# Queries and keys of three retention heads in seven products, tables made late, and a few steps moved

## The chip, the core and the metric

The kernel runs on one NeuronCore of a Trainium2 chip. The metric is the device time of one launch in microseconds (us); smaller is better. TensorE is PE in the rows, its weight loads PEld, VectorE DVE, ScalarE ACT, GpSimd POOL, and SyncE, which issues most transfers, SP.

## What is computed

One decoder layer on 512 tokens of width 1024, batch 1, everything in float32. Two branches read the same normalised input: latent attention with eight heads, and retention with four heads (queries and keys 256 wide, values and gates 512 wide). Their gated sum goes through an output projection, then come a squared-ReLU MLP and a gated embedding.

```python
h = rms_norm(x, norm_mix); proj = h @ w_in
rq, rk, rv, rg, cq, ckv, krope, gr, gm = split(proj)
rq = rope(rq, pos); rk = rope(rk, pos) * 256 ** -0.5
ro = retention(rq, rk, rv)            # causal scores times a decay, per head
a_ret = (rms_norm(ro) * silu(rg)) @ w_br
a_mla = latent_attention(cq, ckv, krope, pos) @ w_bm
x = x + (sigmoid(gr) * a_ret + sigmoid(gm) * a_mla) @ w_o
x = x + square(relu(rms_norm(x) @ w_up)) @ w_down
x = x + sigmoid(rms_norm(x) @ w_ple_gate) * (p @ w_ple)
```

## The kernel before

Features lie on the 128 partitions and tokens along the free side. A float32 product is made of three products in the format fp32r: each operand is split into a high part and a rest, and low by high, high by low and high by high are added in PSUM (`mm3`, all under L169). So each 128x512 product costs three matmuls.

All weights are streamed in chunks, mostly 128x1024 (512 KB). SP loads a chunk into a raw tile `wr_...` (six of them, NRAW), ScalarE copies the high part into `wh_...` (L262), VectorE subtracts to get the rest `wl_...` (L266); three such pairs exist. `load_chunk` does this one chunk ahead of the chunk in use (AHEAD 1), `prepare` issues loads three ahead (PREP 3). The program is a list of steps in a fixed order (`step(key, fn, ...)`); `run_steps` walks it. TensorE and the transfers follow the order in which this is written; on the other engines a scheduler may place instructions in another order, unless an instruction is pinned with `keep_in_program_order`.

Values and gates of retention (`rv`, `rg`), for two heads at a time (a pair `q`), and the MLP are done by a scheme with seven half-size products instead of eight, numbered 1, 7, 2, 6, 5, 4, 3. For it, sums of weight blocks are needed. They are made by transfers: product 7's chunk is loaded by SP, then POOL issues a transfer that adds a second block onto it; for products 6 and 4 POOL adds further blocks onto the same raw tile, which it can do only after `wl_` of the product before has read that tile. Product 5's chunk is likewise a load plus an addition. `XS[p]` holds the matching sums of the input. `seven_out` collects the seven results out of three PSUM chains (a: 1, 6, 5, 3; c: 7, 4; b: 2).

Queries and keys of each head are made by `ret_qk` in four chunks (rq 0, rq 1, rk 0, rk 1), each of 24 matmuls 128x512, then turned by the tables `cr`, `sr` (cosine, sine) on VectorE. `ret_scores` makes scores (`rs`), `ret_attend` the outputs (`ro`) and the sum of squares; `ret_gated` multiplies output, root and gate (four VectorE operations, `o`), `ret_turned` transposes that through PSUM (`ot`, sixteen TensorE transposes) and splits the four PSUM tiles into `rog0h`, `rog0l` and so on (ScalarE, then VectorE); `branch_r` multiplies by `w_br` (`br`). PSUM has eight banks, all handed out by one pool (`B(...)`).

Before retention come the first products (`pA`), latents, eight attention heads, and the products with `w_bm` (`bm`). During attention, chunks of the gate projection (`gm`) serve as fillers: `fill(n)` puts n of them into the list of steps at that place. The tables of retention are made between `pair_stats` and the first head factors:

```python
    step(None, pair_stats, 0)
    fill(2)
    step(None, ret_angles)
    step(None, ret_sincos)
    step(None, head_factor, 0)
```

The MLP begins with `up` chunks in the plain form, then `dn` and `us` chunks in seven products; `up_operand` splits the sums of the normalised input (`xu6h`, `xu2h`, ...) for the later `us` products.

## Time and profile before

| | |
|---|---|
| time before, median of 3 runs | 1102.07 us (1100.86 to 1102.21) |
| the profiled execution, its own time | 1101.0 us |
| its span in the profile | 1099.2 us |
| TensorE busy | 1085.2 us, 99% |
| VectorE busy | 757.9 us, 69% |
| ScalarE busy | 565.8 us, 51% |
| GpSimd busy | 111.1 us, 10% |
| granted TensorE clock, mean | 0.999 |

Times in a trace count from the start of the span; the profiled execution took 1.8 us more than its span, and the median of the runs is 1.1 us above the profiled execution. Matmuls are pipelined and their ends are modelled, so what one costs is the distance from its start to the next start, not its duration.

### The profile page before, as it was taken

To read this page: it belongs to the slowest core of one execution; us is meant where nothing else is said; L and a number is where in the kernel's file an instruction comes from. 1 tells how busy PE (TensorE), PEld (TensorE's weight loads), DVE (VectorE), ACT (ScalarE), POOL (GpSimd) and SP (SyncE) were. 2 spreads that over 40 slices of the span, in tenths; PEclk is the share of its full clock that TensorE was granted. 3 is DMA by queue.
4 is the path that set the end of the run, shared out by engine and by line. 5 is a ranking of instruction groups with operands and counts; after the bars stand their busy time and mean duration, and the time that the engine had idled before them with its cause. 6 is when DMAs were issued, how large, how long until landed. Compare 5 with 4: busy or idle time off the path is not lost. (4 is left out here: it accounts for less than half of the span.)

```text
span 1099.2 us, 14887 instructions
## 1 busy us (share of the span) xinstructions
PE 1085.2 (99%) x5569; PEld 923.3 (84%) x5569; DVE 757.9 (69%) x1176; ACT 565.8 (51%) x817; POOL 111.1 (10%) x145
## 2 busy tenths in 40 slices
PE   9999999999999999999999999999999999999998
PEld 7778888888888888888888888887899899898887
DVE  7697677566774655655465467649869769769784
ACT  7647656444466545344554644426645545546541
POOL 0000000000112001122100100011111111201000
PEclk9999999999999999999999999999999999999999
DMA  7232231356778744498864934694998999979511
GB/s 261 71 120 87 72 107 50 133 199 212 206 190 241 193 157 159 121 196 213 204 205 118 286 126 148 199 305 117 229 267 222 229 272 220 238 217 279 154 47 58
DMA packets 64616, 195.91 MB, mean 178 GB/s; under 512 B 7904, under 2 KB 9312, under 8 KB 64160
## 3 DMA queue, kind: packets, MB, share of 16 engines
q1 hardware_dynamic: 46464, 134.90, 35.7%
q0 software_dynamic: 17936, 60.04, 27.3%
q8 instruction: 44, 0.72, 0.3%
q14 instruction: 28, 0.23, 0.1%
q10 hardware_dynamic: 144, 0.03, 0.0%
HBM read 175.80 MB, written 17.04 MB: 175 GB/s over the span
## 5 line engine op out<-in xcount | busy, mean ns | idle before, releaser
L169 PE MATMUL dn<-wl_dn,ch 128*128 128x512 f32 x224 | 87.7, 391 | 1.5 <-DVE wl_dn L266 1.5
L169 PE MATMUL dn<-wh_dn,cl 128*128 128x512 f32 x224 | 87.7, 391 | 1.4 <-DVE cl L308 0.9
L169 PE MATMUL dn<-wh_dn,ch 128*128 128x512 f32 x224 | 87.2, 389 | 0.0
L262 ACT ACTIVATE wh_up<-wr_up 128x1024 fp32r<-128x1024 f32 x32 | 33.9, 1058 | 44.1 <-PE us L169 13.4
L266 DVE TENSOR_TENSOR wl_up<-wr_up,wh_up 128x1024 fp32r<-128x1024 f32 x32 | 39.1, 1221 | 24.4 <-ACT wh_up L262 24.0
L262 ACT ACTIVATE wh_dn<-wr_dn 128x1024 fp32r<-128x1024 f32 x32 | 33.9, 1059 | 34.1 <-PE us L169 16.5
L169 PEld LDWEIGHTS dn<-wh_dn,cl 128*128 128x128 f32 x224 | 42.1, 188 | 10.5 <-DVE cl L308 1.3
L169 PEld LDWEIGHTS dn<-wl_dn,ch 128*128 128x128 f32 x224 | 42.1, 188 | 10.3 <-DVE wl_dn L266 2.3
L169 PEld LDWEIGHTS dn<-wh_dn,ch 128*128 128x128 f32 x224 | 42.1, 188 | 8.8
L266 DVE TENSOR_TENSOR wl_dn<-wr_dn,wh_dn 128x1024 fp32r<-128x1024 f32 x32 | 39.0, 1220 | 10.7 <-ACT wh_dn L262 10.6
L262 ACT ACTIVATE wh_rv<-wr_rv 128x1024 fp32r<-128x1024 f32 x28 | 29.7, 1059 | 30.6 <-issue 9.9
L262 ACT ACTIVATE wh_rg<-wr_rg 128x1024 fp32r<-128x1024 f32 x28 | 29.6, 1059 | 30.4 <-PE rg L169 12.1
L266 DVE TENSOR_TENSOR wl_rg<-wr_rg,wh_rg 128x1024 fp32r<-128x1024 f32 x20 | 24.5, 1226 | 23.5 <-ACT wh_rg L262 23.4
L224 POOL DMA_DIRECT2D dr_dn<-wstream x24 | 21.9, 957 | 173.2 <-DVE rx L331 95.9
L266 DVE TENSOR_TENSOR wl_dn<-dr_dn,wh_dn 128x1024 fp32r<-128x1024 f32 x24 | 29.3, 1220 | 13.9 <-ACT wh_dn L262 13.9
L266 DVE TENSOR_TENSOR wl_rv<-wr_rv,wh_rv 128x1024 fp32r<-128x1024 f32 x20 | 24.4, 1223 | 16.2 <-ACT wh_rv L262 16.2
L266 DVE TENSOR_TENSOR wl_br<-wr_br,wh_br 128x1024 fp32r<-128x1024 f32 x16 | 19.5, 1221 | 19.7 <-ACT wh_br L262 19.7
L1105 DVE TENSOR_TENSOR d<-d,dn 128x1024 f32<-128x1024 f32 x24 | 29.2, 1217 | 5.4 <-PE dn L169 5.4
L262 ACT ACTIVATE wh_up<-dr_up 128x1024 fp32r<-128x1024 f32 x18 | 19.1, 1062 | 25.9 <-PE dn L169 14.1
L262 ACT ACTIVATE wh_dn<-dr_dn 128x1024 fp32r<-128x1024 f32 x24 | 25.3, 1053 | 13.1 <-PE dn L169 6.5
L262 ACT ACTIVATE wh_br<-wr_br 128x1024 fp32r<-128x1024 f32 x16 | 16.9, 1058 | 21.0 <-issue 12.8
L873 ACT ACTIVATE rt<-br 128x512 f32<-128x512 f32 x24 | 13.9, 594 | 25.8 <-PE br L169 25.8
(1889 smaller groups left out, 3690.2 us busy)
## 6 DMA issues: line engine op xcount, KB each, us to landing
wr_up<-wstream SPq DMA_DIRECT2D x32, 512.0 KB, 5.6
wr_dn<-wstream SPq DMA_DIRECT2D x32, 512.0 KB, 6.9
dr_dn<-wstream POOLq DMA_DIRECT2D x24, 512.0 KB, 9.5
wr_rv<-wstream SPq DMA_DIRECT2D x20, 512.0 KB, 4.1
wr_rg<-wstream SPq DMA_DIRECT2D x20, 512.0 KB, 5.0
dr_up<-wstream POOLq DMA_DIRECT2D x18, 512.0 KB, 9.0
wr_rv<-wstream POOLq DMA_DIRECT2D x16, 512.0 KB, 6.5
wr_rg<-wstream POOLq DMA_DIRECT2D x16, 512.0 KB, 6.9
```

The lines of the kernel that those rows point to most:

```text
L169: return tc.keep_in_program_order(nc.tensor.matmul(*a, **k))
L224: nc.gpsimd.dma_start(raw, chunk(("w", blk, kb, fb, c)), accum_op=ALU.add)
L262: i = ACT(hi, raw, AF.Copy, scale=sign)
L266: TT(lo, raw, hi.bitcast(F32), op=ALU.subtract)
L873: ACT(t, ps, AF.Copy)
L1105: TT(to, to, dps[p], op=ALU.add if sign > 0 else ALU.subtract)
```

## The change

- Queries and keys of heads 1, 2 and 3 (counted from 0) go through the seven products: a head has seven chunks of 24 matmuls 128x256 (`ret_qk7`), with four additions by POOL. Head 0 keeps `ret_qk`. The chunks of heads 1 and 3 stand among the last gate products of their pair.
- In the second pair the first value product (two chunks) comes ahead of the queries and keys of head 2, with `ret_gated` of head 1 cut in two between them; then come products 1 and 7 of `qk`, the transposes of head 1, and products 2 and 6.
- The tables of retention leave the attention part and are made at the beginning of the `bm` part from a second load of the positions; cosine and sine share one tile `tab`. NDYN falls by two.
- Four token tiles `xr` are loaded ahead of their first use there, and each later one four steps ahead.
- One filler chunk is put in behind `mask_parts`; the later ones each move up.
- At the start: 8 matmuls with zeros instead of 9, the first two token tiles on ScalarE's queue, the gains on SP's behind the first, and the first chunk's nine products ordered by kind.
- Conversions of `dn` 0 and `up` 1, and the splits of `up_operand` for products other than 1 and 7, are pinned to the order of the program.

The core of the diff; of the loop over pairs of heads, at its end, the new and the kept lines alone are shown.

```diff
-NDYN, NKEEP, NW, NRAW, NDRAW, AHEAD, PREP, EARLY, PAD = 45, 16, 3, 6, 4, 1, 3, 5, 104
+NDYN, NKEEP, NW, NRAW, NDRAW, AHEAD, PREP, EARLY, PAD = 43, 16, 3, 6, 4, 1, 3, 5, 104
...
-        for key, o in (("rq", O_RQ), ("rk", O_RK)):
+        for key, o in (("rq", O_RQ), ("rk", O_RK)) if h == 0 else ():
...
+            for h in range(1, RH):
+                add(("w", ("qk", h), kb, fb, 0), "w_in", _rng(kb * S, S), _rng((O_RQ, O_RK)[fb] + h * RQK, RQK))
...
-        if key[0] == "a1":
+        if key[0] == "a1" or key[0] == "sw" and key[1] in (("dn", 0), ("up", 1)):
             tc.keep_in_program_order(i)
...
-            ACT(hi, src, AF.Copy)
+            i = ACT(hi, src, AF.Copy)
+            if pin:
+                tc.keep_in_program_order(i)
...
-    for i in range(9):
-        MM(ps, zero[:, 0:P], zero, start=i == 0, stop=i == 8)
+    for i in range(8):
+        MM(ps, zero[:, 0:P], zero, start=i == 0, stop=i == 7)
...
-        tc.keep_in_program_order(nc.sync.dma_start(xs[k], xT[:, k]))
-    nc.scalar.dma_start(gn, gains)
+        tc.keep_in_program_order((nc.sync if k > 1 else nc.scalar).dma_start(xs[k], xT[:, k]))
+        if k == 0:
+            tc.keep_in_program_order(nc.sync.dma_start(gn, gains))
...
-        for n in range(3):
-            mm3(V["pA"][n], cut(w, n * P), xg[k], k == 0, k == 7)
+        if k == 0:
+
+            (wh, wl), (xh, xl) = w, xg[k]
+            for i, (stat, mov) in enumerate(((wl, xh), (wh, xh), (wh, xl))):
+                for n in range(3):
+                    MM(V["pA"][n], stat[:, n * P:n * P + P], mov, start=i == 0, stop=False)
+        else:
+            for n in range(3):
+                mm3(V["pA"][n], cut(w, n * P), xg[k], False, k == 7)
...
-        ang, kf, c_, s_ = T(name + "a"), T(name + "k"), T(name + "c"), T(name + "s")
+        ang, kf = T(name + "a"), T(name + "k")
+        if name == "tr":
+            V["tab"] = dyn.tile([P, 2, S], F32, tag="tab", name="tab", bufs=1)
+            c_, s_ = V["tab"][:, 0], V["tab"][:, 1]
+        else:
+            c_, s_ = T(name + "c"), T(name + "s")
...
-        V["ar"] = trig("tr", V["posf"], cst[:, C_INVR:C_INVR + 1])
+        again, posf = dyn.tile([P, S], I32, tag="t", name="posr"), T("posrf")
+        nc.sync.dma_start(again, pos.partition_broadcast(P))
+        nc.vector.tensor_copy(posf, again)
+        V["ar"] = trig("tr", posf, cst[:, C_INVR:C_INVR + 1])
...
+    def load_x(k):
+        xr.append(T(f"xr{k}"))
+        nc.sync.dma_start(xr[k], xT[:, k])
...
+    def ret_qk7(w, h, p):
+
+        ch, d = CHAIN[p], R[h]
+        if p in (1, 7, 2):
+            qkps[ch] = B(f"qk{h}{p}")
+        ps = qkps[ch]
+        for o in range(2):
+            for k in range(4):
+                mm3(ps[:, o * 256:o * 256 + 256], cut(w, k * 256 + o * P), XS[p][k], p in (1, 7, 2) and o + k == 0,
+                    o == 1 and k == 3, skip_group_check=True)
+        done = seven_out(d.setdefault("qk", {}), p, ps, f"qk{h}_")
+        if not done:
+            return
+        blk, t = done
+        key, cs = ("rq", "rk")[blk % 10 - 1], slice(256 * (blk // 10 - 1), 256 * (blk // 10))
+        a, b = T(f"{key}a{h}{blk}"), T(f"{key}b{h}{blk}")
+        lo_, hi_ = slice(0, 256), slice(256, 512)
+        TT(a.rearrange("p (k c) -> p k c", k=2), t.rearrange("p (k c) -> p k c", k=2), V["tab"][:, :, cs], op=ALU.mult)
+        TT(b[:, lo_], t[:, lo_], V["tab"][:, 1, cs], op=ALU.mult)
+        TT(b[:, hi_], t[:, hi_], V["tab"][:, 0, cs], op=ALU.mult)
+        first = key not in d
+        if first:
+            d[key] = (T(f"{key}u{h}"), T(f"{key}v{h}"))
+        u, v = d[key]
+        TT(u[:, cs], a[:, lo_], a[:, hi_], op=ALU.subtract)
+        TT(v[:, cs], b[:, lo_], b[:, hi_], op=ALU.add)
+        if not first:
+            d[key] = (split(u, f"{key}x{h}"), split(v, f"{key}y{h}"))
+
     def ret_scores(h):
...
-    def ret_gated(h):
+    def ret_gated(h, bs=(0, 1, 2, 3)):
         d = R[h]
-        for b in range(4):
+        for b in bs:
...
-            split(src[:, 2 * c:2 * c + 2], None, scale, hi=hi, lo=lo)
+            split(src[:, 2 * c:2 * c + 2], None, scale, hi=hi, lo=lo, pin=p not in (1, 7))
...
     step(None, mask_parts)
+    fill(1)
     step(None, rotary_out, 0)
...
-    step(None, ret_angles)
-    step(None, ret_sincos)
...
     fill(len(fillers))
+    step(None, ret_angles)
+    for k in range(4):
+        step(None, load_x, k)
     step(None, norm_x, 0)
     step(None, norm_x, 1)
...
+        if n == 0:
+            step(None, ret_sincos)
...
+    def qk(h, *ps):
+        for p in ps:
+            step(("sw", ("qk", h), p, 0), ret_qk7, h, p)
...
     for q in range(RH // 2):
         h = 2 * q
         if q:
+            for c in range(2):
+                step(("sw", ("rv", q), 1, c), ret_seven, "rv", q, 1, c)
+                step(None, ret_gated, h - 1, (2 * c, 2 * c + 1))
+            qk(h, 1, 7)
             step(None, ret_turned, h - 1)
+            qk(h, 2, 6)
+            branch(h - 1, 0)
+            qk(h, 5, 4, 3)
+            branch(h - 1, 1, 2)
+            step(None, ret_scores, h)
+            seven("rv", q, 7, 2, 6)
+            branch(h - 1, 3)
+        else:
+            for key in ("rq", "rk"):
+                for n in range(2):
+                    step((key, h, n), ret_qk, h, key, n)
+            for p, x in ((1, 6), (7, 5), (2, 3)):
+                seven("rv", q, p)
+                step(None, x_operand, x)
+            seven("rv", q, 6)
+            step(None, ret_scores, h)
+        seven("rv", q, 5, 4, 3)
+        seven("rg", q, 1)
+        step(None, ret_attend, h)
+        seven("rg", q, 7, 2, 6)
+        qk(h + 1, 1, 7)
+        seven("rg", q, 5)
+        qk(h + 1, 2)
+        seven("rg", q, 4)
+        step(None, ret_gated, h)
+        qk(h + 1, 6)
+        seven("rg", q, 3)
         step(None, ret_turned, h)
+        qk(h + 1, 5, 4, 3)
+        branch(h, 0, 1)
         step(None, ret_scores, h + 1)
         step(None, odd_v, h + 1)
         branch(h, 2, 3)
         step(None, ret_attend, h + 1)
+    step(None, ret_gated, RH - 1)
```

Three places show how instructions move. Behind head 1's retention outputs, VectorE before (`o13` is the last of the four gated outputs, `rqa20` and `rqb20` head 2's query before rotation, `ot10` the PSUM tile of transposes, `wl_br_1_0` the rest of the branch's first chunk):

```order
L853 SCALAR_TENSOR_TENSOR o13_4341<-o13_4341,ro1_4346,z01_22_3669 128x512
L811 TENSOR_TENSOR rqa20_4395<-rq20_4370,trc_931 128x512
L812 TENSOR_TENSOR rqb20_4396<-rq20_4370,trs_932 128x512
L266 TENSOR_TENSOR wl_br_1_0_4483<-wr_br_1_0_4480,wh_br_1_0_4482 128x1024
L811 TENSOR_TENSOR rqa21_4430<-rq21_4405,trs_932 128x512
L812 TENSOR_TENSOR rqb21_4431<-rq21_4405,trc_931 128x512
L817 TENSOR_TENSOR rqa20_4395<-rqa20_4395,rqa21_4430 128x512
L818 TENSOR_TENSOR rqb20_4396<-rqb20_4396,rqb21_4431 128x512
L313 SCALAR_TENSOR_TENSOR rog10l_4450<-ot10_4444,gn_81,rog10h_4449 128x512
```

VectorE now, from the same `o13` (`wr_qk270` is head 2's raw tile for products 7, 6 and 4):

```order
L905 SCALAR_TENSOR_TENSOR o13_4457<-o13_4457,ro1_4462,z01_22_3671 128x512
L268 TENSOR_TENSOR wl_qk270_4524<-wr_qk270_4480,wh_qk270_4523 128x1024
L268 TENSOR_TENSOR wl_qk220_4556<-wr_qk220_4503,wh_qk220_4555 128x1024
L268 TENSOR_TENSOR wl_qk260_4623<-wr_qk270_4480,wh_qk260_4622 128x1024
L317 SCALAR_TENSOR_TENSOR rog10l_4592<-ot10_4586,gn_81,rog10h_4591 128x512
L317 SCALAR_TENSOR_TENSOR rog12l_4610<-ot12_4604,gn_81,rog12h_4609 128x512
L317 SCALAR_TENSOR_TENSOR rog11l_4601<-ot11_4595,gn_81,rog11h_4600 128x512
L317 SCALAR_TENSOR_TENSOR rog13l_4619<-ot13_4613,gn_81,rog13h_4618 128x512
L268 TENSOR_TENSOR wl_br_1_0_4664<-wr_br_1_0_4661,wh_br_1_0_4663 128x1024
```

And ScalarE now, at that place:

```order
L264 ACTIVATE wh_qk220_4555<-wr_qk220_4503 128x1024
L772 ACTIVATE qk2_11_4553<-qk21_4528 128x512
L264 ACTIVATE wh_qk260_4622<-wr_qk270_4480 128x1024
L772 ACTIVATE qk2_22_4584<-qk27_4559 128x512
L314 ACTIVATE rog10h_4591<-ot10_4586,gn_81 128x512
L314 ACTIVATE rog12h_4609<-ot12_4604,gn_81 128x512
L314 ACTIVATE rog11h_4600<-ot11_4595,gn_81 128x512
L314 ACTIVATE rog13h_4618<-ot13_4613,gn_81 128x512
L264 ACTIVATE wh_br_1_0_4663<-wr_br_1_0_4661 128x1024
```

Before, between `o13` and the first reader of the transposes (`rog10l`) stood rotations and one weight chunk; now three weight chunks stand there, the last of which (`wl_qk260`) reads `wr_qk270` after POOL has added a block onto it, which it may do once `wl_qk270` has read it. On ScalarE `rog10h` stands behind `wh_qk260` in the same way.

At the entry of the MLP's seven products, ScalarE before (`wh_dn011` and `wh_dn070` belong to the second and third `dn` chunk, `f01` is a squared activation):

```order
L985 ACTIVATE f01_6835<-f01_6835 128x1024
L307 ACTIVATE xu6h_7118<-x2n0_6698 128x512
L262 ACTIVATE wh_dn011_6927<-wr_dn011_6849 128x1024
L307 ACTIVATE xu6h_7118<-x2n0_6698 128x512
L307 ACTIVATE xu2h0_7271<-x2n1_6768 128x512
L307 ACTIVATE xu2h1_7272<-x2n1_6768 128x512
L307 ACTIVATE xu5h0_7320<-x2n0_6698 128x512
L307 ACTIVATE xu5h1_7321<-x2n0_6698 128x512
L310 ACTIVATE xu4h0_7427<-x2n1_6768 128x512
L310 ACTIVATE xu4h1_7428<-x2n1_6768 128x512
L262 ACTIVATE wh_dn070_6947<-dr_dn070_6880 128x1024
```

ScalarE now:

```order
L1037 ACTIVATE f01_7167<-f01_7167 128x1024
L264 ACTIVATE wh_dn011_7259<-wr_dn011_7181 128x1024
L264 ACTIVATE wh_dn070_7279<-dr_dn070_7212 128x1024
L1037 ACTIVATE f01_7167<-f01_7167 128x1024
L309 ACTIVATE ch02_7300<-f01_7167 128x1024
L264 ACTIVATE wh_dn071_7304<-dr_dn071_7263 128x1024
```

The eight splits between the two conversions have gone to later places, behind the next chunks' conversions.

Ahead of the first attention head, ScalarE before (`trs`, `trc` are the tables, `kf0` and `kf1` the factors that the first head's scores are multiplied by):

```order
L262 ACTIVATE wh_gm_4_0_1047<-wr_gm_4_0_1045 128x512
L487 ACTIVATE trs_932<-tra_929 128x512
L488 ACTIVATE trc_931<-tra_929 128x512
L613 ACTIVATE kf0_950<-pbk0_945 128x512
L489 ACTIVATE trc_931<-trc_931 128x512
L613 ACTIVATE kf1_957<-pbk1_952 128x512
L262 ACTIVATE wh_v_1_1082<-wr_v_1_1080 128x512
```

ScalarE now:

```order
L264 ACTIVATE wh_gm_4_1_1049<-wr_gm_4_1_1047 128x512
L632 ACTIVATE kf0_952<-pbk0_947 128x512
L632 ACTIVATE kf1_959<-pbk1_954 128x512
L669 ACT_TABLE_LOAD
L669 ACTIVATE p00_961,sums_994<-p00_961,ng_993,hr_887 128x128
```

The three table operations have gone from between the filler's conversion and the factors.

## Rows read from the trace of the kernel before

**Rows 1.** The page's head and its part 1: busy time, share of the span and number of instructions of TensorE.

```profile
span 1099.2 us, 14887 instructions
PE 1085.2 (99%) x5569; PEld 923.3 (84%) x5569; DVE 757.9 (69%) x1176; ACT 565.8 (51%) x817; POOL 111.1 (10%) x145
```

**Rows 2.** What TensorE waited for over the whole span: engine, line and tile that waits, what it waits for; us in total, times, longest.

```profile
PE gm L169 <- DVE wl_gm L266: 1.6, 1, 1.6
PE dn L169 <- DVE cl L308: 0.9, 1, 0.9
```

**Rows 3.** The time line of TensorE: start us, us, engine, line, operation, out<-in, shapes, count, and in brackets the idle time before it with what ended it. The first pair is the step behind the last retention product of head 2, the second pair the transposes of its output, the third two neighbours of the MLP's seven products.

```profile
439.23 0.39 PE L169 MATMUL rq<-xn0h,wl_rq 128*128 128x512 f32 x1
439.46 0.39 PE L169 MATMUL rq<-xn0l,wh_rq 128*128 128x512 f32 x1
...
450.12 1.91 PE L169 MATMUL ot<-cst,o 128*128 128x128 f32 x16
451.78 0.48 PE L169 MATMUL rk<-xn0h,wl_rk 128*128 128x512 f32 x1
...
770.38 0.28 PE L169 MATMUL us<-xu1l,wh_up 128*128 128x256 f32 x1
770.50 0.28 PE L169 MATMUL us<-xu1h,wh_up 128*128 128x256 f32 x1
```

**Rows 4.** The time line of 82 to 101 us on TensorE, ScalarE and VectorE (columns as in rows 3).

```profile
82.48 1.03 PE L169 MATMUL pbk<-cst,hr 128*128 128x128 f32 x8
...
89.62 0.58 ACT L613 ACTIVATE kf<-pbk 128x512 f32<-128x512 f32 x1
90.24 0.29 DVE L644 CUSTOM_DVE_ANT_0 p<-sc,kf 128x128 f32<-128x128 f32 x1 [1.71 <-ACT kf L613]
...
96.36 0.39 PE L169 MATMUL gm<-xg3h,wh_gm 128*128 128x512 f32 x1
97.39 0.66 PE L169 MATMUL pt0a<-cst,p 128*128 128x128 f32 x4 [0.65 <-DVE p L653]
...
99.86 0.28 PE L169 MATMUL sc<-maskr,identr 128*128 128x256 f32 x1
100.94 0.45 PE L169 MATMUL sc<-k1h,q1l 128*128 128x384 f32 x1 [0.81 <-ACT sqk L527]
```

**Rows 5.** The time line of 443 to 453 us on VectorE and ScalarE.

```profile
443.02 2.74 DVE L853 SCALAR_TENSOR_TENSOR o<-o,ro,z 128x512 f32<-128x512 f32 x4
444.87 1.06 ACT L262 ACTIVATE wh_br<-wr_br 128x1024 fp32r<-128x1024 f32 x1 [4.26 <-PE rq L169]
446.88 1.21 DVE L266 TENSOR_TENSOR wl_br<-wr_br,wh_br 128x1024 fp32r<-128x1024 f32 x1
...
451.28 0.67 ACT L310 ACTIVATE rog10h<-ot,gn 128x512 fp32r<-128x512 f32 x1
452.72 0.74 DVE L313 SCALAR_TENSOR_TENSOR rog10l<-ot,gn,rog10h 128x512 fp32r<-128x512 f32 x1
```

**Rows 6.** DMA issues of the whole span: out<-in, the queue that issues, operation, count, KB of each, median us from issue to landing. Those of weight chunks on POOL's queue are the additions onto a chunk already loaded.

```profile
wr_rg<-wstream SPq DMA_DIRECT2D x20, 512.0 KB, 5.0
wr_rv<-wstream POOLq DMA_DIRECT2D x16, 512.0 KB, 6.5
wr_rg<-wstream POOLq DMA_DIRECT2D x16, 512.0 KB, 6.9
dr_dn<-wstream POOLq DMA_DIRECT2D x24, 512.0 KB, 9.5
wr_dn<-wstream POOLq DMA_DIRECT2D x8, 512.0 KB, 5.9
```

**Rows 7.** The time line of 755 to 771 us on ScalarE, VectorE and TensorE.

```profile
759.74 1.14 ACT L310 ACTIVATE xu4h<-x2n 128x512 fp32r<-128x512 f32 x2
760.78 1.04 ACT L262 ACTIVATE wh_dn<-dr_dn 128x1024 fp32r<-128x1024 f32 x1
760.94 0.39 PE L169 MATMUL dn<-wh_dn,ch 128*128 128x512 f32 x1
761.87 0.51 PE L169 MATMUL dn<-wh_dn,cl 128*128 128x512 f32 x1 [0.54 <-ACT wh_dn L262]
762.62 1.21 DVE L266 TENSOR_TENSOR wl_dn<-dr_dn,wh_dn 128x1024 fp32r<-128x1024 f32 x1
763.88 0.50 PE L169 MATMUL dn<-wl_dn,ch 128*128 128x512 f32 x1 [1.50 <-DVE wl_dn L266]
...
769.15 0.39 PE L169 MATMUL dn<-wh_dn,ch 128*128 128x512 f32 x1
770.16 0.39 PE L169 MATMUL us<-xu1h,wl_up 128*128 128x256 f32 x1 [0.62 <-DVE wl_up L266]
```

**Rows 8.** The time line of TensorE's first 8 us.

```profile
1.46 4.21 PE L169 MATMUL zero<-zero 128*128 128x512 f32 x9 [1.46 <-DVE zero L362]
5.46 0.47 PE L169 MATMUL pA<-xg0h,wl_a 128*128 128x512 f32 x1
...
7.92 0.50 PE L169 MATMUL pA<-xg1h,wl_a 128*128 128x512 f32 x1 [0.16 <-ACT xg1h L310]
```

**Rows 9.** Stretches near the end of the span: window, its length, then busy us (count) of TensorE, its weight loads, VectorE, ScalarE and GpSimd, the granted TensorE clock as a share of 2.4 GHz, the DMA share and GB/s.

```profile
1094.00:1096.00 2.00, 0.35 (x3) 0.15 (x2) 1.09 (x3) 0.42 (x1) 0.00 (x0) 1.00 0.19 66
...
1098.00:1099.20 1.20, 0.00 (x0) 0.00 (x0) 0.00 (x0) 0.00 (x0) 0.00 (x0) 0.50 0.00 0
```

More of the change, by code (lines that the diff above doesn't have):

```diff
@@ L495, in angles @@
         nc.vector.tensor_copy(posf, posi)
-        V["posf"] = posf
         V["am"] = trig("tm", posf, cst[:, C_INVM:C_INVM + 1])
@@ L706, in trunk_layer @@
     xr, xn, XS = [], [], {}
+    def load_x(k):
+        xr.append(T(f"xr{k}"))
+        nc.sync.dma_start(xr[k], xT[:, k])
     def norm_x(k):
-        t = T(f"xr{k}")
-        nc.sync.dma_start(t, xT[:, k])
+        t = xr[k]
         STT(t, t, g(G_MIX + k), V["rbc"], op0=ALU.mult, op1=ALU.mult)
-        xr.append(t)
         xn.append(split(t, f"xn{k}"))
@@ L749, in seven_out @@
             to = {1: 11, 7: 22, 6: 21}[p]
-            c[to] = (T if to == 21 or name[0] == "c" else Z)(f"{name}{to}")
+            c[to] = (Z if to != 21 and name[0] == "z" else T)(f"{name}{to}")
             ACT(c[to], ps, AF.Copy, scale=1.0 if p == 7 else -1.0)
@@ L819, in ret_qk @@
             d[key] = (split(a0, f"{key}x{h}"), split(b0, f"{key}y{h}"))
+    qkps = {}
+    def ret_qk7(w, h, p):
[25 more added lines that the diff above has]
+            d[key] = (split(u, f"{key}x{h}"), split(v, f"{key}y{h}"))
     def ret_scores(h):
@@ L1275, in trunk_layer @@
     for n in range(8):
+        if n < 4:
+            step(None, load_x, 4 + n)
         step(("bm", n), branch_m, n)
@@ L1282, in trunk_layer, with seven @@
         step(None, x_operand, p)
-    def qk(h, key, n):
-        step((key, h, n), ret_qk, h, key, n)
+    def qk(h, *ps):
+        for p in ps:
+            step(("sw", ("qk", h), p, 0), ret_qk7, h, p)
+    def seven(kind, q, *ps):
+        for p in ps:
+            for c in range(2):
+                step(("sw", (kind, q), p, c), ret_seven, kind, q, p, c)
     def branch(h, *ks):
-        for k in ks if h >= 0 else ():
+        for k in ks:
             step(("br", h, k), branch_r, h, k)
@@ L1291, in trunk_layer @@
         h = 2 * q
-        qk(h, "rq", 0)
-        qk(h, "rq", 1)
         if q:
+            for c in range(2):
+                step(("sw", ("rv", q), 1, c), ret_seven, "rv", q, 1, c)
+                step(None, ret_gated, h - 1, (2 * c, 2 * c + 1))
+            qk(h, 1, 7)
             step(None, ret_turned, h - 1)
-        qk(h, "rk", 0)
-        branch(h - 1, 0)
-        qk(h, "rk", 1)
-        branch(h - 1, 1)
-        for kind in ("rv", "rg"):
-            for p in (1, 7, 2, 6, 5, 4, 3):
-                for c in range(2):
-                    step(("sw", (kind, q), p, c), ret_seven, kind, q, p, c)
-                if (kind, q) == ("rv", 0) and p in (1, 7, 2):
-                    step(None, x_operand, {1: 6, 7: 5, 2: 3}[p])
-                if (kind, p) == ("rv", 1):
-                    branch(h - 1, 2)
-                    if q:
-                        step(None, ret_scores, h)
-                elif (kind, p) == ("rv", 6):
-                    branch(h - 1, 3)
-                    if not q:
-                        step(None, ret_scores, h)
-                elif (kind, p) == ("rg", 1):
-                    step(None, ret_attend, h)
-                elif (kind, p) == ("rg", 6):
-                    qk(h + 1, "rq", 0)
-                elif (kind, p) == ("rg", 4):
-                    step(None, ret_gated, h)
@@ L1321, in trunk_layer @@
-        qk(h + 1, "rq", 1)
+            qk(h, 2, 6)
[14 more added lines that the diff above has]
+            step(None, ret_scores, h)
@@ L1322, in trunk_layer @@
+        seven("rv", q, 5, 4, 3)
[9 more added lines that the diff above has]
+        seven("rg", q, 3)
         step(None, ret_turned, h)
-        qk(h + 1, "rk", 0)
-        branch(h, 0)
-        qk(h + 1, "rk", 1)
-        branch(h, 1)
+        qk(h + 1, 5, 4, 3)
+        branch(h, 0, 1)
@@ L1330, in trunk_layer @@
         step(None, ret_attend, h + 1)
-        step(None, ret_gated, h + 1)
+    step(None, ret_gated, RH - 1)
     for n in range(8):
```

## The prediction

> **What bounds the kernel now.** I read four views. First the page: TensorE is busy 99% of the span [rows 1], so a microsecond is won only by giving TensorE less to do or by removing one of its pauses. Second, what TensorE waited for [rows 2]: no wait is longer than 1.6 us, and none is at a retention tile. The reader is to see that between the attention heads and the MLP there is nothing to win but work, and much to lose: any pause there is new. Third, the time line around each wait, because what a pause costs is the distance between two matmul starts less their usual distance. That distance is 439.46 - 439.23 = 0.227 us for 128x512 and 770.50 - 770.38 = 0.12 us for 128x256 [rows 3]. Fourth, the issues of transfers with their time to landing [rows 6], since the seven products hang on additions made by transfers.
>
> **The products themselves.** A head's queries and keys were 4 x 24 = 96 matmuls of 0.2267 us, 21.76 us. Now they are 7 x 24 = 168 of 0.120 us, 20.16 us. The 256-wide pitch is that of the MLP's products [rows 3], which have the same operand types. Three heads: 3 x 1.60 = **-4.8 us**. The extra weight conversions, three per head, of 1.06 us on ScalarE and 1.2 us on VectorE [rows 5], fit beside: a chunk lasts 2.88 us on TensorE against 2.72 us for a value chunk today, and those run without a wait.
>
> In heads 1 and 3 the additions have time. Product 5 of the gates is the tightest: its raw tile comes free when product 2's rest has been made, some 2 us ahead of that chunk's start, and six chunks lie between (four of 2.72, two of 2.88 us, 16.6 us). The load takes 5.0, the addition 6.9 [rows 6], the two conversions 2.3, 14.2 us in all, against 18.6. I put nothing down, and keep the distance of some 4 us for the rivals.
>
> **The second pair, values first.** Here a wait is added. Let T0 be the end of head 1's outputs, 439.23 in the trace of before [rows 3]. TensorE then has two value chunks (5.44 us), products 1 and 7 of head 2 (5.76) and the sixteen transposes (451.78 - 450.12 = 1.66): product 2 is due at T0 + 12.9. But by then its PSUM bank is the ninth: two value chains, two chains of head 2 and four transposed tiles hold all eight. It must wait for the last reader of `ot10`, which is `rog10l` on VectorE, and the order shows this behind `wl_qk260`; on ScalarE `rog10h` stands behind `wh_qk260`. Both wait for POOL's addition onto `wr_qk270`, which waits for `wl_qk270`, and that stands behind the four gated outputs. From rows: the gated outputs start at 443.02 and take 2.74 [rows 5], so T0 + 6.5. `wl_qk270` 1.2 us: 7.7. The addition lands after 6.5 us, the median of the 16 on value chunks [rows 6]: 14.2. `wh_qk260` 1.06: 15.3. Then on ScalarE a copy out of PSUM (0.5, an estimate from the 0.58 of `kf` in rows 4, overlapped) and `rog10h` 0.67: 16.5; `wl_qk260` is done at 16.5 too; `rog10l` 0.74 [rows 5]: 17.3. TensorE starts product 2 then, **+4.4 us** late. Bounds: with the fastest median on that queue, 5.9 us, it is +3.8; with the slowest, 9.5 us, +7.4 [rows 6]. I take 6.5, since those additions ran in this very part of the span. What is late behind it: products 6, the other `rog` halves and the branch, all of which have their inputs ready during the same pause, so it is paid once. Everything behind on VectorE and ScalarE is late by the same amount as TensorE, and VectorE is 69% busy overall, so nothing adds.
>
> The Trainium skill ("DMA: Bandwidth & Descriptors", Anatomy of one DMA - SWDGE path) gives about 2.0 us plus bytes over 436e3 per us for a transfer issued by GpSimd, an estimate of 3.2 us for 512 KB. By that the pause would be 1.1 us and the whole sum lower by 3.3. The rows disagree: 5.9 to 9.5 us for additions of that size [rows 6]; I go by the rows.
>
> **Tables late.** `pbk` is done at 83.5, but `kf` runs only at 89.62, behind the table's sines, and the first head's scores wait for it on VectorE until 90.24 [rows 4]. From there the lateness runs to TensorE: 97.39 - 96.36 - 0.23 = 0.80 us ahead of `pt0a` and 100.94 - 99.86 - 0.12 = 0.96 ahead of `sc` [rows 4]. In the order now nothing of the table stands there, and `kf` can start 6 us earlier, far more than both pauses: **-1.8 us**. Bounds: 0, if the next thing on those engines is as late, and -2.6 if a further pause of the same kind goes with them. The table's work moves beside the `bm` products, where TensorE does not wait today; less than the 6.1 us by which `kf` was held up, spread over eight chunks of 24 matmuls 128x512 (5.4 us each), costs nothing, up to +1 if one chunk's rest is pushed past its time.
>
> **Early filler.** The wait for `wl_gm`, 1.6 us [rows 2], stays: the second filler's first half now stands one product earlier on TensorE, but its rest `wl_gm` stands where it was in VectorE's order. 0, between -1.6 and +0.5 (the short product that used to cover part of the wait).
>
> **Pins at the MLP's entry.** TensorE pauses three times: 761.87 - 760.94 - 0.23 = 0.70, 763.88 - 761.87 - 0.23 = 1.78, 770.16 - 769.15 - 0.23 = 0.78, together 3.26 us [rows 7]. The cause is on ScalarE: `wh_dn070` starts at 760.78, behind eight splits of `xu` [rows 7]. Those splits now come later. By hand in the new order: `wh_dn011` is no longer behind the first split, `wh_dn070` can run at 755.7 (when its buffer is released), `wl_dn070` is done at 760.2 and due at 761.07; `wl_dn071` at 763.8, due 763.8; `wl_up110` 766.1, due 766.5; `wl_up111` 769.7, due 769.4, because a copy of `dn` now stands ahead of its high part. So about 0.4 us stays: **-2.8 us**, between -3.3 and 0. The displaced splits, 1.14 us a pair on ScalarE [rows 7], land among `dn` and `us` chunks that wait for nothing today.
>
> **Start.** TensorE's first real product starts at 5.46, and the next pause ends at 7.92 with the second token tile [rows 8]. One zero product less saves up to 0.44 us ((5.46 - 1.46) / 9), but 7.92 is set by landing. **-0.2**, between -0.5 and +0.5 (two token tiles on another queue share the same 16 engines). The token loads four ahead and the smaller pool: 0, no wait there.
>
> **Sum.** -4.8 + 4.4 - 1.8 - 2.8 - 0.2 = -5.2 us. Against the profiled execution, 1101.0, that gives 1095.8. The median of the runs shown lies 1.1 higher, 1102.07, and I state the forecast on it: 1096.9, about **1097 us**, faster by 0.5%. A measurement of this kernel can tell about 0.2%, 2.2 us, from no change.
>
> **The rivals.**
> - *The clock falls in the new pause.* At the end of the span TensorE does its last 0.35 us of work behind 1094 and then stands idle, and from 1098 the granted clock is 0.50, the lower level of 1.2 GHz [rows 9]. A pause of 4.4 us is about as long as that. At the start the nine zero products took 0.44 us each instead of 0.227 [rows 8], so the 4 us until the clock rose did 2 us of work: +2 us. Time: 1099. Against it: the longest pause inside the span, 1.6 us, is no test. The Trainium skill ("TensorE: Matmul & The Clock Gate", The HAM clock gate) says the same, that an idle TensorE falls to 1.2 GHz and needs sustained work to come back.
> - *The pause does not come or is short*, because the addition lands at once or `ot10`'s bank is not the one needed. -4.4: 1092.5. The rows on the queue speak against it.
> - *The moves free nothing*: behind each wait removed (tables, pins) stands another as long. +1.8 + 2.8: 1101.5, no change. For it speaks the 0.4 us that I already find left at the entry; against it the 6 us of room at the tables.
> - *Slower: the additions are late everywhere.* The retention part gets twelve more additions and three more loads. If an addition took 12.2 us, the second pair would lose 10.1 instead of 4.4 (+5.7), and product 5's chain of 5.0 + 12.2 + 2.3 = 19.5 us would pass its 18.6 in two pairs (+1.8): 1104.4. That is the point from which it is slower by over 0.2%; the slowest median on the queue, 9.5, stays below it [rows 6].
>
> **How the numbers follow.** Chances: the forecast 0.43, the clock 0.20, no pause 0.14, moves free nothing 0.15, slower 0.08. The forecast alone reaches from 1095 to 1100 (the bounds of the addition and of the start). The range takes in the first four cases: 1092.4 to 1101.4. Faster by over 0.2% (below 1099.9) are the forecast, most of the clock case and no pause: 0.76. Within 0.2%: 0.16. Slower: 0.08.
>
> **What would show it.** Right: 168 matmuls per head at 0.12 us; a wait of TensorE of about 4.4 us at `qk22`, put down to `rog10l`, ahead of it `wh_qk260` waiting for a transfer issued on POOL; no wait at `pt0a` and `sc` near 97 to 101; at most one short wait between 755 and 771; the `gm` wait still near 1.6 us. Wrong: no wait at `qk22`, or waits in heads 1 and 3 at product 5; a granted clock under 1 around 440 to 460; waits in `bm`.

## The result, and the profile after

The changed kernel takes 1106.69 us (median of 12 runs, 1103.38 to 1111.62) against 1102.07 before: a ratio of 1.0043, 95% interval 1.0034 to 1.0052, so 4.7 us or 0.4% slower. The forecast was 1097.0, faster, with a range up to 1101.4: wrong in size and in sign.

The profiled execution is the slowest of the twelve (1111.62 us), 5 us above the median, so some of the pauses in its rows may be shorter or missing in the others. The head of its page answers to [rows 1]:

```profile
span 1109.7 us, 15413 instructions
PE 1086.3 (98%) x5784; PEld 934.8 (84%) x5784; DVE 776.1 (70%) x1219; ACT 580.3 (52%) x836; POOL 121.7 (11%) x157
```

TensorE is busy 1.1 us longer and the span 10.5 us longer. The waits of TensorE answer to [rows 2]; before, none was over 1.6 us, and none was at a retention tile:

```profile
PE qk L171 <- DVE rog10l L317: 4.6, 1, 4.6
PE us L171 <- DVE wl_up L268: 2.6, 3, 1.5
PE mo L171 <- DVE mx L663: 2.3, 1, 2.3
PE gm L171 <- DVE wl_gm L268: 1.9, 1, 1.9
PE qk L171 <- DVE wl_qk L268: 1.5, 1, 1.5
...
PE ro L171 <- ACT rv11h L309: 1.2, 1, 1.2
...
PE dn L171 <- DVE wl_dn L268: 0.9, 2, 0.5
```

The seven products run at the pitch that was forecast, 391.89 - 391.77 = 0.12 us, in two neighbours of head 1:

```profile
391.77 0.28 PE L171 MATMUL qk<-s61l,wh_qk 128*128 128x256 f32 x1
391.89 0.28 PE L171 MATMUL qk<-s61h,wh_qk 128*128 128x256 f32 x1
```

In heads 1 and 3 no `qk` product waits, as forecast.

Around head 2, in order of time, on POOL, ScalarE, TensorE and VectorE:

```profile
429.00 0.90 POOL L226 DMA_DIRECT2D wr_qk<-wstream  x1 [8.05 <-DVE rv10l L312]
429.57 0.89 POOL L824 DMA_DIRECT2D rv11l<-v1d  x1
...
435.54 0.63 ACT L309 ACTIVATE rv11h<-rv11l 128x512 fp32r<-128x512 f32 x1 [6.19 <-DMA rv11l<-v1d]
436.22 0.51 PE L171 MATMUL ro<-rv11h,atl 128*128 128x512 f32 x1 [1.17 <-ACT rv11h L309]
...
448.36 2.74 DVE L905 SCALAR_TENSOR_TENSOR o<-o,ro,z 128x512 f32<-128x512 f32 x4
451.02 2.35 DVE L268 TENSOR_TENSOR wl_qk<-wr_qk,wh_qk 128x1024 fp32r<-128x1024 f32 x2
452.29 0.39 PE L171 MATMUL qk<-s70h,wl_qk 128*128 128x256 f32 x1 [1.48 <-DVE wl_qk L268]
452.54 0.91 POOL L226 DMA_DIRECT2D wr_qk<-wstream  x1 [9.89 <-DVE wl_qk L268]
...
458.72 1.06 ACT L264 ACTIVATE wh_qk<-wr_qk 128x1024 fp32r<-128x1024 f32 x1 [7.28 <-DMA wr_qk<-wstream]
459.80 1.23 DVE L268 TENSOR_TENSOR wl_qk<-wr_qk,wh_qk 128x1024 fp32r<-128x1024 f32 x1 [6.43 <-ACT wh_qk L264]
460.95 0.74 DVE L317 SCALAR_TENSOR_TENSOR rog10l<-ot,gn,rog10h 128x512 fp32r<-128x512 f32 x1
461.75 0.58 PE L171 MATMUL qk<-xn4h,wl_qk 128*128 128x256 f32 x1 [4.57 <-DVE rog10l L317]
```

Read it from below. TensorE starts product 2 at 461.75, 4.57 us idle, released by `rog10l` at 460.95, which ran behind `wl_qk` at 459.80, behind `wh_qk` at 458.72, which waited for the addition issued at 452.54: the chain of the forecast, link by link. The addition landed in 6.2 us (458.72 - 452.54) against the 6.5 assumed [rows 6]. But above it stand two waits that the forecast did not have. `rv11h` at 435.54 waited for a load that POOL issued at 429.57, behind head 2's addition at 429.00, and TensorE paused 1.17 us for it. And the gated outputs ended at 451.1, so that product 7 waited 1.48 us for `wl_qk`.

The granted clock in the two places behind the long pauses (columns as in rows 9):

```profile
150.00:154.00 4.00, 4.00 (x15) 3.61 (x15) 2.51 (x11) 2.81 (x9) 0.00 (x0) 0.57 0.42 105
460.00:468.00 8.00, 6.25 (x30) 6.26 (x31) 5.49 (x8) 4.25 (x7) 0.88 (x1) 0.57 0.58 131
```

In both it lies between the two levels on the mean: in the first, 4.00 x 0.43 = 1.7 us of full-speed time are lost. In the second the first 1.75 us are still the pause; behind it 27 products follow each other at 0.21 instead of 0.12 us, 2.7 us more with the first step. Over the twelve runs the mean granted clock was 0.994 to 0.997, against 0.999 in the profiled execution of before.

The new wait among the attention heads, on TensorE and VectorE:

```profile
147.17 0.28 PE L171 MATMUL pv<-wh_v,ckv1h 128*128 128x256 f32 x1
149.36 0.28 DVE L663 CUSTOM_DVE_ANT_0 p<-sc,kf 128x128 f32<-128x128 f32 x1
149.80 0.47 PE L171 MATMUL mo<-ath,v10l 128*128 128x512 f32 x1 [2.35 <-DVE mx L663]
```

`mo` follows `pv` at 149.80 instead of 147.17 + 0.12 = 147.29, after VectorE has begun to read the scores (`p<-sc` at 149.36).

The MLP's entry and what follows it, TensorE with the ScalarE and VectorE rows ahead of the last wait, against [rows 7]:

```profile
779.15 0.39 PE L171 MATMUL us<-xu1h,wl_up 128*128 128x256 f32 x1 [0.45 <-DVE wl_up L268]
...
791.20 0.50 PE L171 MATMUL dn<-wl_dn,ch 128*128 128x512 f32 x1 [0.51 <-DVE wl_dn L268]
794.70 0.35 PE L171 MATMUL us<-xu7h,wl_up 128*128 128x256 f32 x1 [0.71 <-DVE wl_up L268]
...
820.67 0.50 PE L171 MATMUL dn<-wl_dn,ch 128*128 128x512 f32 x1 [0.35 <-DVE wl_dn L268]
...
823.51 1.03 ACT L1155 ACTIVATE d<-dn 128x1024 f32<-128x1024 f32 x1 [3.22 <-PE dn L171]
824.44 1.14 ACT L314 ACTIVATE xu4h<-x2n 128x512 fp32r<-128x512 f32 x2
825.48 1.99 ACT L264 ACTIVATE wh_up<-wr_up 128x1024 fp32r<-128x1024 f32 x2
826.56 2.36 DVE L268 TENSOR_TENSOR wl_up<-wr_up,wh_up 128x1024 fp32r<-128x1024 f32 x2 [0.17 <-ACT wh_up L264]
827.84 0.39 PE L171 MATMUL us<-xu2h,wl_up 128*128 128x256 f32 x1 [1.49 <-DVE wl_up L268]
```

The three pauses of 3.26 us in all at the entry have become one of 779.15 - 778.41 - 0.12 = 0.6 (0.4 was forecast; 778.41 is the start of the product before). But there are four later ones: from start to start they cost 0.67, 0.87, 0.51 and 1.65 us, 3.7 in all. The last is read from the rows: `wl_up` waits for `wh_up` at 825.48, which stands behind the two pinned `xu4h` splits, and those behind `d<-dn`, which waits for TensorE.

The start, against [rows 8]:

```profile
1.46 3.78 PE L171 MATMUL zero<-zero 128*128 128x512 f32 x8 [1.46 <-DVE zero L366]
5.90 1.65 PE L171 MATMUL pA<-xg0h,wl_a 128*128 128x512 f32 x3 [0.66 <-ACT xg0h L314]
...
9.91 0.57 PE L171 MATMUL pA<-xg1h,wl_a 128*128 128x512 f32 x1
```

The first nine products take 9.91 - 5.90 = 4.0 us, 0.44 each, the lower clock's pitch; before they took 2.5 us. TensorE stood idle 0.66 us ahead of them, for the first token tile.

### The profile page after: what moved, and what is told of

Read it like the earlier page. It is cut to its first block, busy times and chain, and to the rows that moved or that the text cites. A ratio compares the mean times of both kernels' runs of the same rounds, so it can differ in the third digit from the quotient of the medians.

```text
span 1109.7 us, 15413 instructions
## 1 busy us (share of the span) xinstructions
PE 1086.3 (98%) x5784; PEld 934.8 (84%) x5784; DVE 776.1 (70%) x1219; ACT 580.3 (52%) x836; POOL 121.7 (11%) x157
## 5 line engine op out<-in xcount | busy, mean ns | idle before, releaser
L264 ACT ACTIVATE wh_qk<-wr_qk 128x1024 fp32r<-128x1024 f32 x21 | 22.3, 1062 | 21.4 <-DMA wr_qk<-wstream 9.2
L268 DVE TENSOR_TENSOR wl_qk<-wr_qk,wh_qk 128x1024 fp32r<-128x1024 f32 x15 | 18.3, 1223 | 16.9 <-ACT wh_qk L264 16.9
```

The costliest lines, as they stand in the source:

```text
L264: i = ACT(hi, raw, AF.Copy, scale=sign)
L268: TT(lo, raw, hi.bitcast(F32), op=ALU.subtract)
```

## The experiments

All ratios are to the kernel before, run beside each, with a 95% interval; the changed kernel's own is 1.0043 [1.0034, 1.0052].

**Values first undone.**

```diff
-            for c in range(2):
-                step(("sw", ("rv", q), 1, c), ret_seven, "rv", q, 1, c)
-                step(None, ret_gated, h - 1, (2 * c, 2 * c + 1))
-            qk(h, 1, 7)
+            step(None, ret_gated, h - 1)
+            qk(h, 1, 7, 2)
             step(None, ret_turned, h - 1)
-            qk(h, 2, 6)
             branch(h - 1, 0)
+            qk(h, 6)
+            branch(h - 1, 1)
             qk(h, 5, 4, 3)
-            branch(h - 1, 1, 2)
+            seven("rv", q, 1)
+            branch(h - 1, 2)
```

> The changed kernel with the second pair in another order: queries and keys of head 2 first (products 1, 7, 2, the transposes of head 1, a branch chunk, 6, a branch chunk, 5, 4, 3), then the first value product; all else as changed. Theory A (the waits around head 2 come from values standing first: product 6's addition and the transposed tiles' reader share an in-order queue with it, and the clock falls in the pause): the 4.6 us at qk22, the 1.5 us at product 7 and the lowered clock behind them go, some 8 to 11 us less than the changed kernel in a run like its profiled one, so 1097 to 1100. Rival (the pause belongs to the seven products of head 2 wherever they stand): a wait of 3 to 5 us turns up at another qk product, and the time stays within 2 us of 1106.7.

1.0061 [1.0045, 1.0076], 1108.82 us. The rival came nearer: the pause moved.

```profile
PE br L171 <- DVE rog10l L317: 3.7, 1, 3.7
```

Here TensorE came to the branch directly behind the transposes, and `rog10l` stood behind head 2's rotation on VectorE. So the order of the steps alone does not remove the pause; and since this order has a pause of its own making, it does not tell what values first costs.

**The splits pinned ahead of product 6's conversion.** `wh_qk26` keeps its place on ScalarE, and so do the four splits `rog10h` to `rog13h`.

```diff
-        if key[0] == "a1" or key[0] == "sw" and key[1] in (("dn", 0), ("up", 1)):
+        if key[0] == "a1" or key[0] == "sw" and (key[1] in (("dn", 0), ("up", 1)) or key[1:3] == (("qk", 2), 6)):
...
-            d["rog"].append(split(ps, None, g(G_RET + 4 * h + m), hi=new(f"rog{h}{m}h", F32R), lo=new(f"rog{h}{m}l", F32R)))
+            d["rog"].append(split(ps, None, g(G_RET + 4 * h + m), hi=new(f"rog{h}{m}h", F32R), lo=new(f"rog{h}{m}l", F32R), pin=h == 1))
```

> The changed kernel with head 1's four splits of the transposes and product 6's conversion of head 2 pinned on ScalarE, so that the splits stand ahead of that conversion; all else as changed. Theory A1 (the in-order queues: the bank's reader stood behind a conversion that waits for the addition): the wait at qk22 goes (under 0.5 us) and a shorter one comes at product 6 itself, 2 to 3 us, whose addition lands about 15 us behind the outputs' end plus the lateness of the gates; 2 to 4 us less than the changed kernel, 1103 to 1105. Rival (eight banks are too few there, whatever the order): the wait at qk22 stays over 3 us and the time is that of the changed kernel.

1.0011 [1.0000, 1.0022], 1103.28 us: 3.4 us less than the changed kernel. TensorE's two waits around head 2 now:

```profile
453.99 0.39 PE L171 MATMUL qk<-xn4h,wl_qk 128*128 128x256 f32 x1 [0.30 <-DVE rog10l L317]
...
457.54 0.39 PE L171 MATMUL qk<-s60h,wl_qk 128*128 128x256 f32 x1 [0.41 <-DVE wl_qk L268]
```

0.30 us instead of 4.57, and 0.41 us at product 6. Eight banks are enough; it was the place in the two in-order queues. The values still stand first. Product 6 waits only 0.4 us instead of the 2 to 3 expected, since in this run the loads of `rv1`, and so the gates, were in time.

**Head 1's value tiles loaded by SP.**

```diff
-                nc.gpsimd.dma_start(lo.bitcast(F32), src)
+                nc.sync.dma_start(lo.bitcast(F32), src)
```

> The changed kernel with head 1's four value tiles loaded from SyncE's queue instead of GpSimd's, all else as changed. Theory (GpSimd's in-order queue held these loads behind head 2's addition for product 5, so that head 1's outputs and everything behind them came late): the waits at ro of up to 1.4 us go, the gates come 2 us earlier against the outputs' end, the 1.5 us at product 7 goes; 3 us less than the changed kernel, 1103.7. Rival (the loads are late for another reason, their tiles or the transfer itself): the ro wait stays.

1.0049 [1.0033, 1.0065], no gain. In the profile the waits at `ro` and at product 7 are gone and the one at qk22 is still 4.5 us. But that shows nothing: those two waits are also absent from the profiles of the kernels without filler, without pins and with the old start (below), whose queue is that of the changed kernel. They come and go with the moment at which POOL issues the addition for product 5: 4.5 us ahead of head 1's first `ro` product in the changed kernel's profile (433.53 - 429.00), 6.3 to 6.8 in those three; and the changed kernel's profile is the slowest of twelve. The experiment is inconclusive.

**No early filler.**

```diff
     step(None, mask_parts)
-    fill(1)
```

> The changed kernel without the filler behind the mask parts, all else as changed. Theory B (the filler's shift by one half puts the first half of a gm chunk, which takes a PSUM bank and keeps it, ahead of the attention output mo2, so that mo2 waits for the scores' reader on VectorE): the 2.3 us at mo goes, with the low clock behind it, some 3 to 4 us less, 1103. Rival (the late tables, not the filler, shifted VectorE there): the mo wait stays, time within 1 us of the changed kernel.

1.0024 [1.0015, 1.0033], 1104.66 us: 2.0 us less than the changed kernel. The `mo` wait is gone, and the clock shows 1.00 there; a wait of 0.6 us at `gm`, as before, is back. So it was the filler and not the tables. That it is the PSUM bank is read from the order: the products with one chunk of `gm` are split into two fillers, of which the first takes a bank; before, a second half stood ahead of `mo2`, with the early filler a first half. The bank itself was not tried apart.

**Tables early again.**

```diff
     step(None, pair_stats, 0)
     fill(2)
+    step(None, ret_angles)
+    step(None, ret_sincos)
     step(None, head_factor, 0)
```

> The changed kernel with the retention tables made in their old place ahead of the first attention head, all else as changed. If making them late gave the forecast 1.8 us, the waits at pt0a and sc near 100 us come back, 0.6 to 0.8 us each, and the time is 1.8 us longer, 1108.5, or more where the clock falls. Rival (the filler's shift alone moved the heads clear of the tables): those waits stay away, time within 1 us of the changed kernel.

1.0083 [1.0070, 1.0096], 1111.41 us, 4.7 us more than the changed kernel. The two waits are back:

```profile
PE pt0a L171 <- DVE p L672: 2.0, 1, 2.0
...
PE sc L171 <- ACT sqk L546: 0.8, 1, 0.8
```

The direction was right; with the filler's shift, the wait at `pt0a` is three times that of before [rows 4]. The two waits are 2.8 us; the rest of the 4.7 is not explained.

**No pins**, and **the old start**, each alone.

```diff
-        if key[0] == "a1" or key[0] == "sw" and key[1] in (("dn", 0), ("up", 1)):
+        if key[0] == "a1":
...
-            split(src[:, 2 * c:2 * c + 2], None, scale, hi=hi, lo=lo, pin=p not in (1, 7))
+            split(src[:, 2 * c:2 * c + 2], None, scale, hi=hi, lo=lo)
```

```diff
-    for i in range(8):
+    for i in range(9):
...
-        tc.keep_in_program_order((nc.sync if k > 1 else nc.scalar).dma_start(xs[k], xT[:, k]))
...
+        tc.keep_in_program_order(nc.sync.dma_start(xs[k], xT[:, k]))
+    nc.scalar.dma_start(gn, gains)
...
-        if k == 0:
...
+        for n in range(3):
+            mm3(V["pA"][n], cut(w, n * P), xg[k], k == 0, k == 7)
```

> The changed kernel without the pins of the MLP's entry, all else as changed. If the pins freed what was forecast, this is 2.8 us slower than the changed kernel, 1109.5. If they only move the pauses (0.6 left at the entry, but 0.7, 0.9, 0.5 and 1.6 us later), the three waits of before come back at the entry, the later four go, and the time is that of the changed kernel within 1 us.

> The changed kernel with the start of before (nine zero products, token loads on SyncE's queue, first products token by token), all else as changed. Theory D (the changed start has TensorE stand idle for 0.7 us before the first product, and the clock rises at 9.9 us instead of 5.6): the clock rises by 6 us again and 1 us is won, 1105.7. Rival (the moment at which the clock rises varies by itself): the clock's rise lies anywhere in 5 to 10 us in both, no difference beyond 0.5 us.

Without pins 1.0053 [1.0040, 1.0066]; the intervals overlap. The median, 1107.94, is 1.3 us above the changed kernel, between the two forecasts of this run, so it does not decide between them; best2 without pins (below) does better. With the old start 1.0076 [1.0063, 1.0090], 3.1 us more, which neither theory gave. In its profile the first products came as before (the fifteenth at 9.68, before at 9.74); but behind the 1.9 us wait for `wl_gm` the clock fell once more:

```profile
69.00:73.00 4.00, 4.00 (x11) 3.14 (x12) 2.83 (x5) 0.00 (x0) 0.56 (x1) 0.57 0.58 173
```

**The rest without the seven products**, with and without the early filler; the loop over pairs of heads is that of before:

```diff
-        for key, o in (("rq", O_RQ), ("rk", O_RK)) if h == 0 else ():
+        for key, o in (("rq", O_RQ), ("rk", O_RK)):
...
-    def qk(h, *ps):
...
+    def qk(h, key, n):
+        step((key, h, n), ret_qk, h, key, n)
...
```

> The changed kernel with queries and keys of all heads made as before and the order of the retention part as before; so the late tables, the early filler, the pins, the start and the token loads alone. The forecast's terms for these (tables -1.8, pins -2.8, start -0.2, filler 0) would give 4.8 us less than before, 1096.9. If the filler's bank costs 2.5 to 4 us and the pins only move the pauses, it is between 2 less and 2 more than before, 1100 to 1104.

> As rest, without the filler behind the mask parts: late tables, pins, start and token loads alone. If the filler is the part that costs, 2 to 4 us less than rest: 1098 to 1100. Rival (rest is held up by the pins or the start): same as rest within 1 us.

1.0037 [1.0023, 1.0050] and 1.0002 [0.9994, 1.0011]; 1105.26 and 1101.65 us. So the filler costs 3.6 us here, and late tables, pins, start and token loads together win nothing. In the second one the waits at `pt0a` and `sc` are gone, but these stand where there were none or are as before:

```profile
PE us L169 <- DVE wl_up L266: 2.4, 3, 1.5
PE gm L169 <- DVE wl_gm L266: 1.6, 1, 1.6
```

Where the time goes is seen from the first products of the MLP (`up`) and of what follows it (`pw`), before and then in the second one:

```profile
710.69 0.39 PE L169 MATMUL up<-x2g0h,wl_up 128*128 128x512 f32 x1
1012.36 0.39 PE L169 MATMUL pw<-pph,wl_ple 128*128 128x512 f32 x1
...
710.21 0.39 PE L169 MATMUL up<-x2g0h,wl_up 128*128 128x512 f32 x1
1012.88 0.39 PE L169 MATMUL pw<-pph,wl_ple 128*128 128x512 f32 x1
```

The MLP lasts 302.7 us instead of 301.7, where the pins were to win 2.8.

**Product 6 behind the branch, and all mends together.** (`qk(h, 2); branch(h - 1, 0); qk(h, 6, 5, 4, 3)`, splits ahead of its conversion, tiles by SP, no early filler.)

> Head 1's value tiles on SyncE's queue, its splits ahead of head 2's product 6 conversion, product 6 behind the first branch chunk, and no filler behind the mask parts; all else as changed. If the three causes named (in-order queues around head 2, GpSimd's queue, the filler's bank) are all, the pauses at ro, qk and mo go with the lowered clock behind them: the changed kernel's 15 us above its work less about 11, 1096 to 1098, faster than before by 0.4 to 0.5%. Rival (the pauses move to the branch chunk or to product 5): 1101 to 1104.

1.0017 [1.0007, 1.0026], 1103.02 us: the rival. ScalarE and TensorE at the new pause:

```profile
463.62 1.06 ACT L268 ACTIVATE wh_qk<-wr_qk 128x1024 fp32r<-128x1024 f32 x1 [4.03 <-DMA wr_qk<-wstream]
464.59 0.58 ACT L776 ACTIVATE qk<-qk 128x512 f32<-128x512 f32 x1
465.22 0.58 PE L171 MATMUL qk<-s50h,wl_qk 128*128 128x256 f32 x1 [3.39 <-ACT qk L776]
```

The mechanism of qk22 again: product 5 must wait until product 6's sum is copied out of its PSUM chain (`qk<-qk` at 464.59), and that copy stands on ScalarE behind the conversion of product 4 (463.62), which waits for its addition.

**Product 6 left ahead of the branch**, then the MLP's product 4 unpinned as well:

```diff
-            split(src[:, 2 * c:2 * c + 2], None, scale, hi=hi, lo=lo, pin=p not in (1, 7))
+            split(src[:, 2 * c:2 * c + 2], None, scale, hi=hi, lo=lo, pin=p not in (1, 7, 4))      # best3 alone
```

> The changed kernel with head 1's splits pinned ahead of head 2's product 6 conversion, head 1's value tiles on SyncE's queue and no filler behind the mask parts; product 6 stays ahead of the branch. With the wait at qk22 and the one at mo gone and nothing in their place, the products' 4.8 us show: 4 to 6 us less than the kernel without seven products in retention (rest_nofill) and 1097 to 1099 in all. Rival (the seven products cost as much in waits as they save, wherever the first wait is mended): within 1 us of rest_nofill.

> As best2, with the splits of the MLP's product 4 no longer pinned, so that they stand ahead of a weight conversion less. The 1.5 us wait for wl_up near 818 us goes: 1 to 2 us less than best2. Rival (another split or landing takes its place): the same as best2.

0.9960 [0.9948, 0.9972] and 0.9945 [0.9933, 0.9958]; 1096.61 and 1095.82 us. Both beat the kernel before and the changed one; their times do not tell the two apart. Against the rest without filler, best2 is 0.42% faster: 4.6 us, the products' 4.8. In best3 these are among the longest waits; the 1.5 us at `us` is gone, and the clock is 1.00 up to 1093 us:

```profile
PE gm L171 <- DVE wl_gm L268: 1.6, 1, 1.6
...
PE us L171 <- DVE wl_up L268: 0.9, 2, 0.5
...
PE qk L171 <- DVE wl_qk L268: 0.5, 1, 0.5
```

**Start and pins in a kernel without long pauses.**

> best3 with the start of before. Undoing the start in the changed kernel made it 3 us slower though its first products came 1 us earlier in the profile; behind it the clock fell once more, after the wait for wl_gm near 69 us. If the start by itself costs or wins, the same 3 us show here (1098.8). If it only decided whether a later pause met a fall of the clock, then without long pauses the old start is 0 to 1 us faster than best3: 1094.8 to 1095.8.

> best2 without the pins of the MLP's entry. If they only move pauses (3.3 us at the entry against 0.6 there and 3.2 later), the same time as best2 within 0.7 us, 1096 to 1097.3. If they win something that the other pauses hid, 2 us more: 1098.6.

0.9958 [0.9945, 0.9970] against 0.9945 [0.9933, 0.9958], and 0.9947 [0.9933, 0.9960] against 0.9960 [0.9948, 0.9972]. No difference in either: the start by itself is worth nothing that can be told, and the pins neither.

The profiles say the same. From `up` to `pw` the MLP lasts 302.2 to 304.9 us in the eleven kernels with all pins, 303.2 and 303.3 in the two without pins, and 300.2 and 300.8 in the two with product 4 unpinned: it is the pinned `xu4h` splits that cost there. Why it lasts longer than before without pins as well stays open. The first `pcq` product, which follows the `pA` products, starts anywhere from 22.3 to 24.7 us in the thirteen profiles with the new start, and at 23.7, 23.7 and 24.0 in the three with the old one.

## Why the prediction was wrong

By the times, the miss of 9.7 us has three parts. Tables, pins, start and token loads alone, in the rest without filler, come to +0.2 us where -4.8 was forecast. The early filler costs 3.6 us where nothing was put down. Products and second pair together come to +0.7 us (1.0043 against 1.0037) where -0.4 was. Term by term:

| step | forecast us | what the runs showed |
|---|---|---|
| the products | -4.8 | right: -4.6 (best2 against the rest without filler) |
| second pair, the pause at qk22 | +4.4 | right: 4.6 idle, by the chain named |
| second pair, all else | 0 | in the profile 1.8 at `ro`, 1.6 at product 7, 2.7 by the clock; without the first two, some 6.5 to 7.5 for the pair in three other profiles |
| tables late | -1.8 | right: both waits gone, and `pcq` to the first `bm` product 1.4 shorter in the rest without filler |
| early filler | 0 | +2.0 to +3.6 |
| pins | -2.8 | nothing in the times: 2.7 won at the entry, 3.7 lost behind it in the profile |
| start | -0.2 | +1.0 in the profile, where the clock rose late; nothing in the times of best3 |

For the pins the step that failed is the last sentence, that the displaced splits land among chunks that wait for nothing. They waited for nothing since the splits had been done early. And the additions for the later `dn` products are issued when the earlier chunk has been converted; that TensorE, with the entry sooner, ran up to them (0.67 and 0.87 us) is read from the order and not tried apart. The rival "the moves free nothing" held for the pins and not for the tables. (The range ends 0.1 us below the sum of that rival, 1101.5, which it was to take in; that changes nothing.)

"0" for the early filler was a step too short: I followed its rest `wl_gm` on VectorE, and that wait indeed stayed (1.9 us). What moved was the parity of the halves: which of them stands ahead of `mo2` decides whether TensorE waits there; that it is for a PSUM bank was argued and not shown.

The clock was named but left out of the sum. It stood among the rivals at 0.20, because I judged it by one pause alone, the 4.4 us. It fell behind that pause (2.7 us), and also behind a pause of 2.35 us at `mo` (1.7 us), which I had not foreseen: it fell behind `mo` in all eight profiles that have this wait, and not there in the eight that have not. The Trainium skill ("TensorE: Matmul & The Clock Gate", The HAM clock gate) has an idle TensorE fall to 1.2 GHz; the rows agree, with the 0.57 in both windows. The 5.0 us lost by tables, pins and start are not the clock's: in the rest without filler its mean is 0.999 to 1.000 in every run.

Taken from the changed kernel one at a time, the splits bring 0.32%, the filler 0.19% and the loads nothing, 0.5% together; all three at once bring 0.83%, some 9 us, and the clock then stays at 1.00 until the last products are done. What makes the whole more than the parts, by some 3.5 us that are hardly clear of the noise of four ratios, stays open. The clock does not explain it: in the profiles the splits and the filler each take away the fall behind their own pause and leave the other.

In the second pair the step that fell short is the end of the gated outputs, taken from the rows of before as T0 + 6.5. They hang on the squares of head 1's outputs, and those on loads in POOL's queue, which now stand behind head 2's addition for product 5. I had looked at POOL's queue only for the additions. In the changed kernel's profile (T0 is 442.34) they end at T0 + 8.8, in the three other profiles at T0 + 6.9 to 7.3, so it is a cost that comes in some executions. That the pause at qk22 came out at 4.6 is in that profile partly luck: the chain ended 2.1 us later than forecast, at T0 + 19.4, and TensorE itself came 1.6 us late. Without pins, where product 7 did not wait, it is 4.7.

The Trainium skill's estimate for an addition, 3.2 us ("DMA: Bandwidth & Descriptors", Anatomy of one DMA), would have made the pause 1.1 us; it was 4.6, and the addition took 6.2. The choice of the row over that estimate was right. The rival that forecast a slower kernel got the sign by another road: its additions of 12.2 us did not come.

Not settled: why the old start made the changed kernel 3.1 us slower. In best3, without long pauses, it makes no difference, which fits that the start only shifts where the clock falls behind later pauses; one profile each does not show that. Nor is it settled what makes POOL issue that addition late in some executions, and what the waits at `ro` and product 7 cost on the mean.

## What to carry to other kernels

Where a conversion waits for a transfer in an in-order queue, look at what stands behind it there and whether it frees a PSUM bank; here a pin that puts the bank's reader ahead was worth more than another order of steps. Cost a pause of TensorE with the clock's fall behind it when it is as long as those that brought one here: behind every pause of 2.3 to 5.0 us in these profiles the clock fell. Before work is moved away from one wait, ask what the work now does for free where it stands.
